# The RWKV branch prepared chunk by chunk without GpSimd, and another spread of the modulation tiles

## The chip, the core and the metric

The kernel runs on one core of a Trainium2 chip. A core has a matrix engine (TensorE, PE in the profile, with its weight loads as PEld), a vector engine (VectorE, DVE), an activation engine (ScalarE, ACT), GpSimd (POOL), and SyncE (SP), on which this kernel issues its transfers. Each engine works through its own queue in order; semaphores make one wait for another. The metric is the device time of one execution in microseconds (us); less is better.

## What is computed

Two layers of a transformer over 256 tokens of width 1024, batch 1, in float32. The first has stick-breaking attention and retention side by side; the second has a modulated norm, a mixer of latent attention (MLA) and an RWKV-7 recurrence joined by gates, and a PEER feed-forward over 16384 experts. Of the second layer the change touches these lines:

```python
mod = silu(c) @ w_ada + b_ada                     # 6 vectors of 1024: shifts, scales, gates
h = modulate(rms_norm(x, norm_mix), sh1, sc1)
proj = h @ w_in                                   # q_a, kv_a, k_rope, rwkv_in, gate_logits
...
p = p + (prev(p) - p) * mu                        # token_shift: the token before, mixed in
r, k, v, wd, ad, gd = split(p)
decay = exp(-exp(-softplus(-(decay_base + tanh(wd) @ w_decay_up)) - 0.5))
a = sigmoid(aaa_base + ad @ w_aaa_up)
kk = normalised(k * k_k);  k = k * (1 + (a - 1) * k_a);  b = kk * a
for t in range(S):                                # rwkv7_scan, per head
    state = state * w[t] - (state @ kk[t]) b[t]^T + v[t] k[t]^T
    y[t] = state @ r[t]
y = group_norm(y) + sum(r * k * r_k) * v          # the "bonus" term
o_rwkv = (y * g) @ w_o_rwkv
...
x = x + gt1 * ((sigmoid(gl[0]) * o_mla + sigmoid(gl[1]) * o_rwkv) @ w_out)
x = x + gt2 * peer(modulate(rms_norm(x, norm_ffn), sh2, sc2))
```

## The kernel before

**Weights.** Activations lie transposed (features on the 128 partitions, 256 tokens along the row). Weights come in tiles of 512 KB: `stream` (L76) issues the transfer on SP, and `halves` (L60) splits each tile in two halves (128x1024 to two of 128x512) and each of those into a high part (`whi`, a cast on ScalarE, L69) and a low part (`wlo`, a subtraction on VectorE, L71, or on GpSimd where `eng` says so, L73). `mm3` (L94 to L98) makes one product of three matmuls: high by high, high by low, low by high. `proj_t` (L101) runs whole projections in chunks of 256 output columns: 48 matmuls of 256 columns and two tiles a chunk. Its result in PSUM is `pj`; the narrow projections are `pn`, those of the gate logits `gj`.

**Order.** The program is written as Python generators, and a scheduler orders each engine's queue from it; `after(g, a, b)` is a hint that a is to stand behind b. In block 2, the loop over `rwkv` (L1073 on) advances three others at each of its yields: `mla` by `NML`, `gate_logits` (64 yields of 6 matmuls) by `NGT`, and the modulation by `NADA`. So gate matmuls fill the places where the recurrence waits.

**The modulation** (`load_mod`, L472) streams 48 tiles `adaw` of 128x1024, each weighed and summed by one VectorE instruction (L486, with its accumulator read). `keep_pace(g, rate)` lets so many of them go out per chunk. Block 1 does 21 of them, block 2 the other 27, partly while the recurrence runs, partly in its three output projections.

**The RWKV branch** (`rwkv`, L510). `shifted` (L523) copies a chunk's result to a buffer with a zero column ahead (`shb`, ScalarE), subtracts the two views (`shd`, GpSimd, L529), and mixes on VectorE (L532). All six chunks of k, r and v are projected first; then come the normalised key (`kkn`, `kk`), `bb` (L616 on GpSimd, L645), the key's weight (L624, `rwk`), the bonus (`bon` L628, matmul `bonp` L632), and the decays folded in (L643 to L646). Then `ntp` (transposes, L656), `mps` and `aps` (products within a chunk of 64 tokens, L674, L681), `mvp`. The triangular systems are inverted in five levels of two halves, ten steps: `bl` (mask product on GpSimd, L714), `zp` = X·bl (PE), Z (copy on ScalarE, L727), `yp` and `xp` (PE), X and Y (subtractions on VectorE, L733, L734). Then the states (`rhs`, `sap`, `ypp`, `u`) and the group norm, which ends in `orh` and `orl`, high and low part of the branch's output. MLA's queries, keys, scores and sums are `qh`, `mkh`, `qkp`, `sc`, `s`, `pp`, `ops`; its output `omh`, `oml`.

**The end of block 2.** Three projections, of MLA's output, of `orh`/`orl`, and of the merged `m2h`/`m2l`, then the norm ahead of the feed-forward (`sq`, `sqa`, `rms`, `nt`, `h3h`). Each chunk of them calls `keep_pace(g, 1)`.

In block 1, the four retention heads (`ret_head`, L387) are issued in a row behind the attention heads.

Of the kernel before, what the change touches and what calls it, by code (L numbers as in the profile page):

```python
# [100 lines left out]
def proj_t(g, w, xh, xl, chunks, nk=8, name="pj", eng=(None,)):  # L101

    nc = g.nc
    for i in chunks:
        bank = g.acc.tile([P, 2, T], F32, tag="acc", name=name)
        for k0, n, hi, lo in stream(g, w[i], nk, eng=eng):
            for c in range(2):
                cs = slice(c * P, (c + 1) * P)
# [4 lines left out]
        g.pm = i.ins
        yield bank
# [129 lines left out]
ADA_RATE = [0.5, 0.5, 0.5, 0, 0.5, 0.5, 0.5, 0, 0.5, 0.5]  # L244


def block1(g, a, xT):
    nc = g.nc
    with ExitStack() as es:
# [173 lines left out]
        turn, heads = {}, []  # L423
        for h in range(6):
            if h < 4:
                heads.append(ret_head(h, turn))
            for gen in reversed(heads):
                next(gen, None)
# [11 lines left out]
        obh, obl = b8("obh", F32R), b8("obl", F32R)  # L440
        gated(3, av, oah, oal)
# [9 lines left out]
        for i, bank in enumerate(proj_t(g, a["w_branch_sb"], oah, oal, range(4))):  # L451
            keep_pace(g, 0.75)
# [3 lines left out]
        for i, bank in enumerate(proj_t(g, a["w_branch_ret"], obh, obl, range(4))):  # L456
            keep_pace(g, 0.75)
# [5 lines left out]
        for i, bank in enumerate(proj_t(g, a["w_out"], mh, ml, range(4))):  # L463
            keep_pace(g, 0.75)
# [46 lines left out]
def rwkv(g, a, hh, hl, cp, b4, wk, og, ol):  # L511
# [60 lines left out]
    table(g, EXPLN)  # L572
    kT, rT, vT = t4("rwk"), t4("rwr"), t4("rwv")
    shifted(a["w2_rkv"], (2, 3), 4, [kT[:, i, :] for i in range(4)])
    shifted(a["w2_rkv"], (0, 1), 0, [rT[:, i, :] for i in range(4)])
    shifted(a["w2_rkv"], (4, 5), 8, [vT[:, i, :] for i in range(4)])
# [907 lines left out]
```

## Time and profile before

| | us |
|---|---|
| median of 3 runs (1485.04 to 1487.40) | 1486.97 |
| the profiled execution | 1486.97 |
| its span (first to last instruction) | 1485.1 |
| TensorE busy | 1423.0 (96%) |
| VectorE busy | 1127.4 (76%) |
| ScalarE busy | 795.6 (54%) |
| GpSimd busy | 122.0 (8%) |

The span lies 1.87 us under the execution's time. TensorE's granted clock is given as a share of 2.4 GHz: 1.00 is full, and a stretch at 1.2 GHz counts as 0.50, so that busy time multiplied by the mean clock is what the same matmuls take at full clock. The program's places in time: block 1 up to about 360 us; the first `lor` matmul (the decay's second layer) at 382.2; `ntp` at 441.6; the first `zp` at 467.3; the first matmul on `omh` at 592.0, on `orh` at 607.2; the last on `m2h`/`m2l` at 650.5; the first on `h3h` at 659.6. From there to the end it is the feed-forward.

### The profile page before, as it was taken

The page shows a single profiled execution, that of the slowest core. Times are in us where ns is not written, and L with a number is a line of the kernel's source. Part 1 is how long each engine was busy: PE and PEld are TensorE (multiplying, and loading weights), DVE is VectorE, ACT ScalarE, POOL GpSimd, SP SyncE. Part 2 cuts the span into 40 slices and gives each one's busy share as a digit, 9 for nine tenths or more (in the row PEclk, how much of TensorE's full clock was granted, in tenths as well). Part 3 has the DMA queues.
Part 4 walks back from the last instruction along what each step waited for, and adds up shares of the span by engine and source line. Part 5 has one row for each costly group of instructions (what it writes and reads, how often), then busy time and mean ns, then how long its engine had stood idle before and what let it go on. Part 6 is the DMA issues. An engine that isn't in the chain of part 4 may idle for free.

```text
span 1485.1 us, 29346 instructions
## 1 busy us (share of the span) xinstructions
PE 1423.0 (96%) x11284; PEld 1324.6 (89%) x11284; DVE 1127.4 (76%) x2411; ACT 795.6 (54%) x1606; POOL 122.0 (8%) x99
## 2 busy tenths in 40 slices
PE   7999999998988999789999998999999999999997
PEld 6999989998977888779999998999998888888886
DVE  8768678688677764988998898989996666666665
ACT  6655557545663445445555555555445555555553
POOL 3012012000153422000000000000000000000001
PEclk9999999999989999889999999999999999999999
DMA  7656526775640343755555554454445566666564
GB/s 252 213 173 194 187 79 204 228 257 187 190 134 18 107 143 100 235 186 177 172 177 182 183 171 145 141 158 155 159 151 172 189 192 193 196 193 194 194 192 135
DMA packets 73723, 256.46 MB, mean 173 GB/s; under 512 B 9328, under 2 KB 10992, under 8 KB 73584
## 3 DMA queue, kind: packets, MB, share of 16 engines
q1 hardware_dynamic: 73584, 254.60, 53.5%
q8 instruction: 88, 1.44, 0.4%
q14 instruction: 51, 0.42, 0.1%
HBM read 253.52 MB, written 1.05 MB: 171 GB/s over the span
## 4 chain that ended last, share of the span: by engine, by line
PE 53%; DVE 1%; issue 0%; POOL 0%; POOLq 0%
PE dn L96 8%; PE dn L98 8%; PE dn L97 8%; PE upp L1307 8%; PE upp L1308 8%; PE upp L1311 8%; PE gps L1280 2%; PE pj L97 1%; PE pj L98 1%; PE pj L96 1%; PE sps L1144 0%; DVE wlo L71 0%; DVE eq L1272 0%; DVE gt L1274 0%; POOL y L1357 0%
## 5 line engine op out<-in xcount | busy, mean ns | idle before, releaser
L69 ACT CAST whi<-eraw 128x512 fp32r<-128x512 f32 x512 | 311.1, 620 | 346.0 <-PE upp L1308 152.0
L71 DVE TENSOR_TENSOR wlo<-eraw,whi 128x512 fp32r<-128x512 f32 x512 | 346.8, 690 | 168.7 <-ACT whi L69 107.8
L69 ACT CAST whi<-wraw 128x512 fp32r<-128x512 f32 x336 | 206.2, 618 | 183.4 <-PE pj L97 98.5
L96 PE MATMUL dn<-h3h,whi 128*128 128x256 f32 x1024 | 293.7, 287 | 0.0
L98 PE MATMUL dn<-h3h,wlo 128*128 128x256 f32 x1024 | 291.8, 285 | 0.0
L97 PE MATMUL dn<-h3l,whi 128*128 128x256 f32 x1024 | 290.9, 284 | 0.0
L71 DVE TENSOR_TENSOR wlo<-wraw,whi 128x512 fp32r<-128x512 f32 x304 | 212.5, 712 | 80.9 <-ACT whi L69 75.9
L97 PEld LDWEIGHTS dn<-h3l,whi 128*128 128x128 f32 x1024 | 197.5, 193 | 0.0
L96 PEld LDWEIGHTS dn<-h3h,whi 128*128 128x128 f32 x1024 | 197.5, 193 | 0.0
L98 PEld LDWEIGHTS dn<-h3h,wlo 128*128 128x128 f32 x1024 | 197.3, 193 | 0.0
L1308 PE MATMUL upp<-whi,wl 128*128 128x512 f32 x512 | 158.9, 390 | 0.0
L1311 PE MATMUL upp<-wlo,wh 128*128 128x512 f32 x512 | 157.9, 390 | 0.0
L98 PE MATMUL pj<-hh,wlo 128*128 128x256 f32 x496 | 141.1, 286 | 2.5 <-DVE wlo L71 2.5
L96 PE MATMUL pj<-hh,whi 128*128 128x256 f32 x496 | 141.2, 286 | 2.2 <-ACT hh L58 1.5
L97 PE MATMUL pj<-hl,whi 128*128 128x256 f32 x496 | 141.5, 286 | 1.0 <-DVE hl L59 0.9
L1307 PE MATMUL upp<-whi,wh 128*128 128x512 f32 x512 | 138.6, 391 | 0.0
L1311 PEld LDWEIGHTS upp<-wlo,wh 128*128 128x128 f32 x512 | 96.1, 188 | 20.1
L1308 PEld LDWEIGHTS upp<-whi,wl 128*128 128x128 f32 x512 | 95.9, 188 | 19.6
L1307 PEld LDWEIGHTS upp<-whi,wh 128*128 128x128 f32 x512 | 95.8, 188 | 19.6
L96 PEld LDWEIGHTS pj<-hh,whi 128*128 128x128 f32 x496 | 95.7, 193 | 3.1 <-ACT hh L58 1.7
L98 PEld LDWEIGHTS pj<-hh,wlo 128*128 128x128 f32 x496 | 95.3, 193 | 3.5 <-DVE wlo L71 3.3
L97 PEld LDWEIGHTS pj<-hl,whi 128*128 128x128 f32 x496 | 95.5, 193 | 2.1 <-DVE hl L59 1.9
(477 smaller groups left out, 2825.2 us busy)
## 6 DMA issues: line engine op xcount, KB each, us to landing
eraw<-in_e_down_dram SPq DMA_DIRECT2D x128, 512.0 KB, 4.0
eraw<-in_e_up_dram SPq DMA_DIRECT2D x128, 512.0 KB, 4.5
wraw<-in_w_in_dram SPq DMA_DIRECT2D x80, 512.0 KB, 4.1
adaw<-in_w_ada_dram SPq DMA_DIRECT2D x48, 512.0 KB, 5.0
wraw<-in_w_out_dram SPq DMA_DIRECT2D x16, 512.0 KB, 4.7
wraw<-in_w_gate_dram SPq DMA_DIRECT2D x16, 512.0 KB, 4.0
wraw<-in_w_query_dram SPq DMA_DIRECT2D x16, 512.0 KB, 4.2
wraw<-in_w_rkv_dram SPq DMA_DIRECT2D x12, 512.0 KB, 4.5
```

The lines of the kernel that those rows point to most:

```text
L69: nc.scalar.copy(hi[:, :m], raw[:, o:o + m])
L71: nc.vector.tensor_tensor(lo[:, :m], raw[:, o:o + m], hi[:, :m], op=ALU.subtract)
L96: nc.tensor.matmul(out, lh, rh, start=start, stop=False)
L97: nc.tensor.matmul(out, lh, rl, start=False, stop=False)
L98: return nc.tensor.matmul(out, ll, rh, start=False, stop=stop)
L1280: nc.tensor.matmul(ps[:, t, :], eq[:, 0, pr, :, o], gt[:, i, pr, :, o], start=i == 0, stop=i == 1)
L1307: nc.tensor.matmul(o, wh[:, ts], hi, start=J == 0, stop=False)
L1308: nc.tensor.matmul(o, wl[:, ts], hi, start=False, stop=False)
L1311: nc.tensor.matmul(up_ps[2 * tt + d0 // 4], wh[:, ts], lo, start=False, stop=J == NJ - 1)
```

## The change

1. `shifted` keeps no buffer: ScalarE writes (1 − mu) times the chunk out of PSUM, VectorE adds mu times the token before, also out of PSUM. It is a generator now: k, r and v are prepared in stages between chunks (`k_stage`, `r_stage`, `v_stage`), and `behind` puts the small matmuls (`lor`, `kkn`, `bonp`) behind the middle of the chunk then running.
2. GpSimd has no work left in block 2's mixer. Seven `shd` go away; `bb`, ten `bl`, the 32 `wlo` halves of the gate logits and the first X and Y products (four on GpSimd, now in quarters) go to VectorE. The tile A and its mask go away.
3. `ADA_RATE` and the rates in block 1's projections change: 31 modulation tiles there, not 21. Block 2 does 14 in the recurrence (rates 0.5 and 0.4 after a start without any), none in the first two output projections, 3 in the last.
4. Block 1's retention heads are issued between the chunks that make block 1's gates.
5. `NGT` gives 42 gate matmuls ahead of `ntp` (78 before), 72 between `ntp` and `zp` (none before), and six after each `zp` and six after each `xp` (before: twelve after each `zp`).

```diff
-ADA_RATE = [0.5, 0.5, 0.5, 0, 0.5, 0.5, 0.5, 0, 0.5, 0.5]
+ADA_RATE = [0.5, 0.5, 0.75, 0.25, 0.75, 0.75, 0.5, 0.25, 1, 1]
...
+                next(ret, None)
...
         for i, bank in enumerate(proj_t(g, a["w_branch_sb"], oah, oal, range(4))):
-            keep_pace(g, 0.75)
+            keep_pace(g, 1)
...
         for i, bank in enumerate(proj_t(g, a["w_out"], mh, ml, range(4))):
-            keep_pace(g, 0.75)
+            keep_pace(g, 0.5)
...
         for b, bank in enumerate(proj_t(g, w, hh, hl, chunks)):
-            buf = wk.tile([P, 2, T + 1], F32, tag="shb", name="shb")
-            nc.vector.memset(buf[:, :, 0:1], 0.0)
-            nc.scalar.copy(buf[:, :, 1:], bank)
-            d = wk.tile([P, 2, T], F32, tag="t512", bufs=4, name="shd")
-            nc.gpsimd.tensor_tensor(d, buf[:, :, 0:T], buf[:, :, 1:], op=ALU.subtract)
             for j in range(2):
                 i = b * 2 + j
-                nc.vector.scalar_tensor_tensor(dsts[i], d[:, j, :], g.vec[:, o_mu + i0 + i:o_mu + i0 + i + 1],
-                                               buf[:, j, 1:], op0=ALU.mult, op1=ALU.add)
+                nc.scalar.activation(dsts[i], bank[:, j, :], AF.Copy, scale=mu1[:, i0 + i:i0 + i + 1])
+                nc.vector.scalar_tensor_tensor(dsts[i][:, 1:T], bank[:, j, 0:T - 1],
+                                               g.vec[:, o_mu + i0 + i:o_mu + i0 + i + 1], dsts[i][:, 1:T],
+                                               op0=ALU.mult, op1=ALU.add)
+            yield b * 2
...
+    next(k_chunks)
+    k_stage(0)
+    r_chunks = shifted(a["w2_rkv"], (0, 1), 0, [rT[:, i, :] for i in range(4)])
+    next(r_chunks)
+    k_stage(2)
+    next(r_chunks)
+    r_stage(0)
+    v_chunks = shifted(a["w2_rkv"], (4, 5), 8, [vT[:, i, :] for i in range(4)])
+    next(v_chunks)
+    r_stage(2)
     yield
...
+    next(v_chunks)
+    v_stage(0)
+    v_stage(2)
     yield
...
             bl = wk.tile([P, 8, 64], F32, tag="bl", bufs=2, name="bl")
-            nc.gpsimd.tensor_tensor(bl, MB[tt][:, :, 0:64], lvl[:, l, :].unsqueeze(1).broadcast_to([P, 8, 64]),
+            nc.vector.tensor_tensor(bl, MB[tt][:, :, 0:64], lvl[:, l, :].unsqueeze(1).broadcast_to([P, 8, 64]),
                                     op=ALU.mult)
...
-NGT = [4, 4, 4, 2] + [2, 0] * 10 + [2] * 11 + [4, 4]
-
-NADA = [0] * 8 + [0.5] * 27 + [0] * 2
+NGT = [4, 4] + [2] * 6 + [1, 1] * 10 + [2, 1] + [1, 2, 1] * 3 + [4, 5]
+
+NADA = [0] * 8 + [0.5] * 20 + [0.4] * 11 + [0] * 2
...
-        for k0, n, hi, lo in stream(g, a["w2_gate"][i], eng=(nc.gpsimd,)):
+        for k0, n, hi, lo in stream(g, a["w2_gate"][i]):
...
         for i, bank in enumerate(proj_t(g, a["w_o_mla_2"], omh, oml, range(4), nk=4)):
-            keep_pace(g, 1)
...
         for i, bank in enumerate(proj_t(g, a["w_o_rwkv_2"], orh, orl, range(4), nk=4)):
-            keep_pace(g, 1)
...
         for i, bank in enumerate(proj_t(g, a["w_out_2"], mh, ml, range(4))):
-            keep_pace(g, 1)
+            keep_pace(g, 0.75)
```

**Order on TensorE ahead of the recurrence.** The bonus matmul and what follows it, before:

```order
3090 L1049 MATMUL gj<-h2h,whi 128x256
3091 L1052 MATMUL gj<-h2l,whi 128x256
3092 L1053 MATMUL gj<-h2h,wlo 128x256
3093 L632 MATMUL bonp<-bon,c_4662 128x512 x2
3094 L656 MATMUL ntp<-perm,bb 128x128 x8
3095 L656 MATMUL ntp<-perm,rwk 128x128 x8
3096 L656 MATMUL ntp<-perm,rwv 128x128 x8
```

and after the change (`pj` there is the last chunk of v):

```order
3034 L97 MATMUL pj<-h2l,whi 128x256
3035 L98 MATMUL pj<-h2h,wlo 128x256
3036 L949 MATMUL cqp<-perm,qn 128x128 x3
3037 L663 MATMUL bonp<-bon,c_4692 128x512 x2
3038 L1080 MATMUL gj<-h2h,whi 128x256
3039 L1083 MATMUL gj<-h2l,whi 128x256
3040 L1084 MATMUL gj<-h2h,wlo 128x256
```

Before, all gate matmuls of this place stood ahead of the bonus, and `ntp` right behind it; now it stands behind the last chunk of v, and 18 gate matmuls lie between it and `ntp`.

**Order on VectorE in the recurrence**, some two steps of it, before:

```order
478 L984 TENSOR_TENSOR s<-sc,cau 128x512
479 L733 TENSOR_TENSOR X<-X,xp 128x512
480 L734 TENSOR_TENSOR Y<-Y,yp 128x512
481 L990 TENSOR_REDUCE m<-s 128x4
482 L486 SCALAR_TENSOR_TENSOR adaw,perm<-adaw,silc 128x1024
483 L994 RECIPROCAL ri<-sm 128x4
484 L995 TENSOR_TENSOR s<-s,ri 128x512
485 L733 TENSOR_TENSOR X<-X,xp 128x512
486 L734 TENSOR_TENSOR Y<-Y,yp 128x512
```

and after:

```order
551 L495 SCALAR_TENSOR_TENSOR adaw,perm<-adaw,silc 128x1024
552 L764 TENSOR_TENSOR X<-X,xp 128x512
553 L765 TENSOR_TENSOR Y<-Y,yp 128x512
554 L59 TENSOR_TENSOR oml<-ops,omh 128x2x128
555 L1015 TENSOR_TENSOR s<-sc,cau 128x2x128
556 L745 TENSOR_TENSOR bl<-MB_5551,c_4692 128x512
557 L1021 TENSOR_REDUCE m<-s 128x2
558 L171 TENSOR_SCALAR gm<-gj 128x512
559 L71 TENSOR_TENSOR wlo<-wraw,whi 128x512
560 L1025 RECIPROCAL ri<-sm 128x2
561 L1026 TENSOR_TENSOR s<-s,ri 128x512
562 L495 SCALAR_TENSOR_TENSOR adaw,perm<-adaw,silc 128x1024
```

Between one pair of X and Y and the next there now stand a `bl`, a `wlo` and a modulation tile on the same queue.

**Order on VectorE from the group norm to `orl`**, before:

```order
617 L486 SCALAR_TENSOR_TENSOR adaw,perm<-adaw,silc 128x1024
618 L71 TENSOR_TENSOR wlo<-wraw,whi 128x512
619 L1092 TENSOR_TENSOR gm<-gm,pj 128x512
620 L814 TENSOR_SCALAR yb<-yb,perm 128x256 x2
621 L71 TENSOR_TENSOR wlo<-wraw,whi 128x512
622 L817 TENSOR_TENSOR yb<-yb,gt 128x512
623 L486 SCALAR_TENSOR_TENSOR adaw,perm<-adaw,silc 128x1024
624 L71 TENSOR_TENSOR wlo<-wraw,whi 128x512
625 L1092 TENSOR_TENSOR gm<-gm,pj 128x512
626 L71 TENSOR_TENSOR wlo<-wraw,whi 128x512
627 L816 TENSOR_TENSOR yb<-yb,bon 128x512
628 L59 TENSOR_TENSOR orl<-yb,orh 128x512
```

and after:

```order
699 L843 TENSOR_TENSOR yb<-yb,gnr 128x512
700 L71 TENSOR_TENSOR wlo<-wraw,whi 128x512
701 L845 TENSOR_SCALAR yb<-yb,perm 128x256 x2
702 L1122 TENSOR_TENSOR gm<-gm,pj 128x512
703 L71 TENSOR_TENSOR wlo<-wraw,whi 128x512
704 L847 TENSOR_TENSOR yb<-yb,bon 128x512
705 L848 TENSOR_TENSOR yb<-yb,gt 128x512
706 L71 TENSOR_TENSOR wlo<-wraw,whi 128x512
707 L1122 TENSOR_TENSOR gm<-gm,pj 128x512
708 L843 TENSOR_TENSOR yb<-yb,gnr 128x512
709 L71 TENSOR_TENSOR wlo<-wraw,whi 128x512
710 L59 TENSOR_TENSOR orl<-yb,orh 128x512
```

No modulation tile stands in this chain any more; the instructions of the chain itself are the same.

## Rows read from the trace of the kernel before

**Rows 1.** The page: busy time of each engine, and VectorE's undisturbed low halves.

```profile
PE 1423.0 (96%) x11284; PEld 1324.6 (89%) x11284; DVE 1127.4 (76%) x2411; ACT 795.6 (54%) x1606; POOL 122.0 (8%) x99
...
L71 DVE TENSOR_TENSOR wlo<-eraw,whi 128x512 fp32r<-128x512 f32 x512 | 346.8, 690 | 168.7 <-ACT whi L69 107.8
```

**Rows 2.** Windows: length, busy (count) of PE PEld DVE ACT POOL, clock, DMA.

```profile
382.20:441.60 59.40, 52.28 (x399) 48.37 (x399) 43.22 (x69) 37.50 (x81) 23.76 (x16) 0.93 0.50 155
441.60:467.27 25.67, 21.73 (x301) 18.51 (x300) 20.43 (x57) 9.69 (x24) 7.52 (x6) 0.89 0.02 8
467.27:592.00 124.73, 119.09 (x1746) 103.78 (x1747) 77.71 (x173) 62.08 (x146) 42.13 (x30) 1.00 0.35 109
592.00:607.20 15.20, 12.52 (x100) 11.84 (x98) 15.12 (x27) 9.43 (x16) 0.00 (x0) 1.00 0.63 210
607.20:625.20 18.00, 14.98 (x108) 14.78 (x109) 16.01 (x29) 6.63 (x11) 0.00 (x0) 0.81 0.70 228
625.20:650.50 25.30, 23.50 (x182) 23.00 (x181) 22.22 (x41) 11.83 (x20) 0.00 (x0) 0.93 0.73 251
650.50:659.60 9.10, 2.22 (x11) 1.26 (x10) 7.80 (x19) 2.78 (x7) 0.67 (x1) 0.78 0.64 202
...
680.00:1485.00 805.00, 792.23 (x5468) 729.22 (x5466) 623.39 (x1435) 419.05 (x873) 4.15 (x3) 0.99 0.54 174
```

**Rows 3.** Waits of TensorE from 360 to 660: total, times, longest (us).

```profile
PE bonp L632 <- DVE bon L628: 6.1, 1, 6.1
PE pj L96 <- ACT h3h L58: 5.0, 1, 5.0
...
PE pj L97 <- DVE orl L59: 3.0, 1, 3.0
PE pj L96 <- ACT orh L58: 2.7, 1, 2.7
PE mvp L696 <- DVE A L683: 2.6, 1, 2.6
PE qkp L969 <- DVE mkh L963: 2.2, 2, 1.3
...
PE pj L97 <- DVE m2l L59: 1.7, 1, 1.7
PE qkp L969 <- DVE qh L884: 1.7, 2, 1.0
```

**Rows 4.** Groups of GpSimd by line: busy us, mean ns, idle before.

```profile
L73 POOL TENSOR_TENSOR wlo<-wraw,whi 128x512 fp32r<-128x512 f32 x32 | 45.5, 1426 | 66.8 <-ACT whi L69 64.9 <-PE gj L1053 1.5
L714 POOL TENSOR_TENSOR bl<-MB,c 128x512 f32<-128x512 f32 x10 | 13.8, 1381 | 37.7 <-PE zp L721 18.2 <-DVE ssq L945 15.5 <-DVE MB L676 4.0
...
L616 POOL TENSOR_TENSOR bb<-kk,al 128x1024 f32<-128x1024 f32 x1 | 3.4, 3442 | 0.8 <-DVE kk L613 0.8
```

**Rows 5.** Groups of VectorE by line and shape from 360 to 600.

```profile
L995 DVE TENSOR_TENSOR s<-s,ri 128x512 f32<-128x512 f32 x6 | 6.6, 1104 | 0.1
...
L645 DVE TENSOR_TENSOR bb<-bb,en 128x1024 f32<-128x1024 f32 x1 | 2.3, 2269 | 2.3 <-POOL bb L616 2.3
...
L646 DVE TENSOR_TENSOR rwk<-rwk,en 128x1024 f32<-128x1024 f32 x1 | 1.2, 1210 | 0.0
```

**Rows 6.** Timeline of VectorE at three modulation tiles: start, length, [idle before].

```profile
602.23 1.23 DVE L486 SCALAR_TENSOR_TENSOR adaw<-adaw,silc 128x1024 f32<-128x1024 f32 x1
603.37 0.09 DVE L486 DVE_READ_ACCUMULATOR adaw<-adaw,silc 128x1 f32 x1
...
650.13 1.23 DVE L486 SCALAR_TENSOR_TENSOR adaw<-adaw,silc 128x1024 f32<-128x1024 f32 x1
...
654.91 1.22 DVE L486 SCALAR_TENSOR_TENSOR adaw<-adaw,silc 128x1024 f32<-128x1024 f32 x1 [0.95 <-DMA adaw<-in_w_ada_dram]
```

**Rows 7.** Windows, columns as in rows 2: the densest transfers of block 1.

```profile
320.00:340.00 20.00, 20.00 (x170) 20.00 (x168) 18.02 (x32) 10.31 (x17) 0.00 (x0) 1.00 0.82 266
```

**Rows 8.** The tile zp: the copy that reads it (min/median/max ns, first and last start).

```profile
L727 ACT COPY Z<-zp x10: 570/586/591, 468.5 to 530.5; 128x512 f32<-128x512 f32 x10
```

More of the change, by code (lines that the diff above doesn't have):

```diff
@@ L413, in ret_head @@
                 if j == 0:
-                    after(g, i.ins, turn[1])
+                    after(g, i.ins, g.pm)
             r = wk.tile([P, T], F32, tag="t256", bufs=3, name="rr")
@@ L421, in ret_head, with ret_heads @@
                                                op0=ALU.mult, op1=ALU.mult)
[L423 to L428, printed above, removed]
+        def ret_heads():
+            heads = []
+            for h in range(6):
+                if h < 4:
+                    heads.append(ret_head(h))
+                for gen in reversed(heads):
+                    next(gen, None)
+                yield
         def gated(i0, x, hi, lo):
@@ L440, in block1 @@
         obh, obl = b8("obh", F32R), b8("obl", F32R)
+        ret = ret_heads()
+        next(ret)
         gated(3, av, oah, oal)
@@ L557, in rwkv, with behind @@
     load(g, eye, a["c_eye"])
-    load(g, slow, a["c_slow"])
     nc.vector.memset(smask, 1.0)
     nc.vector.memset(smask[:, ::64], 0.0)
+    kT, bb = t4("rwk"), t4("bb")
+    k_chunks = shifted(a["w2_rkv"], (2, 3), 4, [kT[:, i, :] for i in range(4)])
+    next(k_chunks)
+    def behind(i):
+        after(g, i.ins, g.mid)
     sg, al = t4("sgm"), t4("al")
@@ L567, in rwkv @@
                 c = c0 + j
-                nc.tensor.matmul(ps[:, j, :], up[r0:r0 + 64, c * P:(c + 1) * P], wdad[r0:r0 + 64, :], start=True, stop=True)
+                behind(nc.tensor.matmul(ps[:, j, :], up[r0:r0 + 64, c * P:(c + 1) * P], wdad[r0:r0 + 64, :],
+                                        start=True, stop=True))
             for j in range(2):
                 act(g, dst[:, c0 + j, :], ps[:, j, :], AF.Sigmoid, bias=col(g, nm, c0 + j))
+    ka1 = wk.tile([P, 4], F32, tag="ka1", bufs=1, name="ka1")
+    o = VEC["k_a_2"][0]
+    nc.vector.tensor_scalar(ka1, g.vec[:, o:o + 4], -1.0, 1.0, op0=ALU.mult, op1=ALU.add)
+    kh = t4("kh")
+    for c in range(4):
+        nc.scalar.activation(kh[:, c, :], al[:, c, :], AF.Identity, scale=col(g, "k_a_2", c), bias=ka1[:, c:c + 1])
     table(g, EXPLN)
[L573 to L576, printed above, removed]
     cu = t4("cu")
@@ L606, in rwkv @@
         ps = g.aux.tile([P, 2, T], F32, tag="aux", name="kkn")
-        nc.tensor.matmul(ps, bones, sq, start=True, stop=True)
+        behind(nc.tensor.matmul(ps, bones, sq, start=True, stop=True))
+        rn = wk.tile([P, 2, T], F32, tag="t512", bufs=4, name="rn")
+        nc.vector.tensor_scalar(rn, ps, 1e-24, None, op0=ALU.max)
+        act(g, rn, rn, AF.Ln)
+        act(g, rn, rn, AF.Exp, scale=-0.5)
+        kk = wk.tile([P, 2, T], F32, tag="kk", bufs=1, name="kk")
+        for j in range(2):
+            nc.vector.scalar_tensor_tensor(kk[:, j, :], kT[:, c + j, :], col(g, "k_k_2", c + j), rn[:, j, :],
+                                           op0=ALU.mult, op1=ALU.mult)
@@ L630, in rwkv, with v_stage @@
-    for c in range(0, 4, 2):
+        nc.vector.tensor_tensor(kh[:, cs, :], kh[:, cs, :], en[:, cs, :], op=ALU.mult)
+    def v_stage(c):
         ps = g.aux.tile([P, 2, T], F32, tag="aux", name="bonp")
-        nc.tensor.matmul(ps, bones, bon[:, c:c + 2, :], start=True, stop=True)
+        behind(nc.tensor.matmul(ps, bones, bon[:, c:c + 2, :], start=True, stop=True))
         nc.vector.tensor_tensor(bon[:, c:c + 2, :], ps, vT[:, c:c + 2, :], op=ALU.mult)
-    yield
-    kr = b4.tile([P, 4, 4, 2, 64], F32, tag="b8s", bufs=1, name="kr")
```

102 lines of the change are left out of this document (47 added, 55 removed).

## Prediction

> **What bounds the kernel now.** First the page's busy line [rows 1]: TensorE is busy 96% of the span, VectorE 76%, GpSimd 8%. That is a matrix-bound kernel, and a change that removes no matmul can only win where TensorE stands still or runs slowly. So the second view is the windows by stage [rows 2]; for each stage I multiply TensorE's busy time by the granted clock, which is what its matmuls take at full clock, and set it against the stage's length. From 680 us on, 792.2 × 0.99 = 784 of 805: little to win, and the change does not touch it. Three stages of block 2 are different:
> - `lor` to `ntp`: 52.28 × 0.93 = 48.6 of 59.40, so 10.8 us lost;
> - `ntp` to `omh` (two rows): 21.73 × 0.89 + 119.09 = 138.4 of 150.40, 12.0 lost;
> - `omh` to `h3h` (four rows): 12.52 + 14.98 × 0.81 + 23.50 × 0.93 + 2.22 × 0.78 = 48.2 of 67.60, 19.4 lost.
>
> That is 42 us in all. The third view, TensorE's waits [rows 3], says for whom: one of 6.1 us ahead of `bonp` in the first stage, the A, `mkh` and `qh` waits (2.6 + 2.2 + 1.7 = 6.5) in the second, `orh`, `orl`, `m2l`, `h3h` (2.7 + 3.0 + 1.7 + 5.0 = 12.4) in the third. The rest is slow clock: the low clocks of rows 2 stand in the very stages that have a long wait.
>
> **Part 1: preparation in stages (`lor` to `ntp`).** Before, the chain k to `kk` to `bb` to `bon` runs after the last chunk of v, and GpSimd is in it: `bb` takes 3.44 us there, and the VectorE instruction that follows takes 2.27 where its twin takes 1.21 [rows 4, 5]. The gate matmuls run out and TensorE stands 6.1 us. In the new order the bonus products of r stand on VectorE while v's chunks run on TensorE (two chunks of 48 matmuls, at the pace of rows 7, 20.00/170 = 0.118 us each, 11 us), so the 6.1 us go, and with them most of the slow clock that follows (52.28 − 48.6 = 3.7 us). What is late next: the first chunk of r. Ahead of its low halves VectorE has the four scans of the decay, two whole-width instructions and two half-width ones; at 0.69 a 512-wide one at most [rows 1] and 1.21 a whole one [rows 5] that is 4 × 0.69 + 2 × 1.21 + 2 × 0.69 = 6.6 us, against one chunk of cover (5.7 us) and two or three low halves that must come before TensorE can start. I take a wait of 2 to 3 us there. Of the 10.8 lost, about 4 stay: gain 7. Bounds: the wait costs nothing and the clock stays high, 10; it is twice as long and slows the clock again, 4.
>
> **Part 2: the recurrence (`ntp` to `omh`).** VectorE takes over here ten `bl`, some 28 of the 32 gate low halves (42 of the gate's 384 matmuls come ahead of `ntp`, and a half serves 12) and the first products. Rows 1 give 0.69 for the 512-wide instruction that takes GpSimd 1.38 to 1.43 [rows 4]: 10 × 0.69 + 28 × 0.69 + about 3 = 29 us more on VectorE. What it gets back is the time by which its instructions are stretched while GpSimd runs: the six `s` products cost 1.104 us [rows 5] where the like costs 0.69, so 2.5 in all. GpSimd runs 36 instructions here [rows 2]; if half of them hold up one VectorE instruction by half their 1.4 us, that is 13, an estimate that I take. Its busy time goes from 20.43 + 77.71 = 98 to about 114 of 150 us [rows 2]: 76%, not a bound by the sum, though it is an in-order queue. Modulation tiles are the same load here (13 before, 14 now). Then the fillers. The copy Z that separates `zp` from `yp` takes 0.586 us [rows 8] and a hand-over; twelve gate matmuls (1.4 us) covered it, six (0.7) just do or fall short by up to 0.3 us, ten times: up to 3 lost. The other six now cover `xp` to X. For it: the 72 gate matmuls among `mps`, `aps` and `mvp` fill just the stretch in which A, `mkh` and `qh` were waited for [rows 3] and the clock was 0.89 [rows 2]. Of 12.0 lost I let 10 remain: gain 2. Bounds: half of it goes, +6; VectorE's queue holds up the chain by 0.8 us in each of ten steps, −6 (with the 2 of gain).
>
> What these rows show, VectorE instructions with two inputs in SBUF stretched beside a reading GpSimd, is also a rule of the Trainium skill (SBUF — State Buffer, Who interferes with whom): the two share a port pair, and the loser blocks for the whole instruction. The trace agrees (2.27 against 1.21), and by that rule all of the stretch goes with GpSimd's work, as assumed.
>
> **Part 3: the end of block 2 (`omh` to `h3h`).** Nothing hides VectorE here: in 592.0 to 607.2 it is busy 15.12 of 15.20 us [rows 2], and its queue from group norm to `orl` holds four modulation tiles; one costs 1.14 us from its start to that of its accumulator read [rows 6]. In the new order none stands there. With three fewer ahead of `orh` it comes 3.4 us earlier, which ends its 2.7 us of wait; with four fewer the first `orl` comes 4.6 earlier, and TensorE, which by then has done its two matmuls on `orh`, waits 1.3 us for it and no more. Together 5.7 become 1.3: 4.4 gained. The clock of 0.81 behind these waits cost 14.98 × 0.19 = 2.8 us; I count it as gone. Four tiles ahead of `m2l` go too, and with them its 1.7 us and the 0.93 clock (23.50 × 0.07 = 1.6). In the norm two tiles [rows 6] stand in the chain: at 650.13 ahead of the last x update (1.14), at 654.91 ahead of `nt`, with a wait for its transfer (0.95 + 1.22, of which I take 1.25, since `nt` needs the last sum as well). In the new order the last tile comes before that update and none before `nt`: 2.4. Sum 4.4 + 2.8 + 1.7 + 1.6 + 2.4 = 12.9; I take 12.5. Bounds: all and the norm's wait shrinks by the clock too, 14.5; the slow clock stays, 8.
>
> **Part 4: block 1.** Ten more tiles there: 10 × 1.22 us of VectorE, beside a TensorE that runs without loss at 320 to 340 with VectorE busy 18.0 of 20 [rows 7], and 5.2 MB more of transfers. In the branch projections the need at rate 1 is three tiles of 0.524 MB in 48 × 0.118 = 5.7 us, 276 GB/s; rows 7 show 266 with no loss, at 0.82 of the engines' time. So it just fits: 0, bounds −4 and +3. The tiles are issued on SP ahead of weights, so a late one holds up what is queued behind it. The retention heads still stand in one block on TensorE, a gate chunk or two later, hundreds of matmuls ahead of their use: nothing.
>
> **Sum.** 7 + 2 + 12.5 + 0 = 21.5. The profiled execution took 1486.97 us, span 1485.1 and 1.87 around it, and is itself the median. 1486.97 − 21.5 = 1465.5.
>
> **The rivals.**
> - *Only the end gains.* Preparation and recurrence trade GpSimd's waits for waits in VectorE's longer queue, r's first chunk above all: parts 1 and 2 cancel, 1486.97 − 12.5 = 1474.5. For it: VectorE would be busy 76% on average, more in the steps. Against: `bonp`'s wait is one of order, not of load.
> - *Block 1 runs out of transfer rate.* At 251 GB/s, the densest of rows 2, a chunk needs 6.3 us in place of 5.7; over 16 chunks 9 us: 1474.5 as well. Against: rows 7.
> - *The stretch is not GpSimd's doing.* Then VectorE gets nothing back, is busy 127 of 150 us, and the recurrence loses 8: 1486.97 − 7 − 12.5 + 8 = 1475.5. Against: L645 beside L646.
> - *The recurrence hangs on VectorE: slower.* In each of the ten steps a `bl` (0.69), a `wlo` (0.69) and a modulation tile (1.22) stand on one queue between X and X; if all of it lies in the chain, 2.6 × 10 = 26 us are lost: 1486.97 − 7 − 12.5 + 26 = 1493.5. It decides from about 2 us a step (19.5 / 10). For it: X and Y wait behind what is queued ahead whoever needs it. Against: the two halves alternate, so that a late X has the other half's step as cover.
>
> On this last one a page speaks against the change: the Trainium skill (Perfetto Trace Analysis, Optimizing Scalar/DVE Operations) has it that a saturated VectorE may be relieved by moving work to GpSimd, and adds that the shared port may take that back. By it the reverse move costs where VectorE is the limit; no stage between `ntp` and `omh` shows it saturated before.
>
> **How the numbers follow.** Forecast 0.52, only the end 0.18, block 1 0.12, no relief 0.06, recurrence slower 0.09, anything else 0.03. Low end: the best bounds, 10 + 6 + 14.5 + 3 = 33.5, so 1453. High end: the middle rivals and some more, 1480; the slower case lies outside. A measurement of this kernel tells about 0.2% (3 us) from no change; faster than that 0.87, within it 0.04, slower 0.09.
>
> **What would show it.** Right: no wait ahead of `bonp`, `lor` to `ntp` in about 52 us; `omh` to `h3h` in about 55 with no wait above 2 us but the norm's; `wlo` on VectorE at 0.69 there and `s` near 0.7; block 1 at its old length. Wrong: TensorE waiting for X, Y or `bl` in most steps between 465 and 530, weight waits in block 1's projections, or an `orh` as late as before.

## The result, and the profile after

The changed kernel takes 1462.75 us (median of 4, 1460.88 to 1464.86) against 1486.01 for the kernel before beside it: a ratio of 0.9843, 95% interval 0.9831 to 0.9854. Forecast was 1465.5, range 1453 to 1480. The profiled execution took 1462.46, span 1460.6, so 24.5 us less than the profiled span before.

The page's busy line [rows 1] now reads

```profile
PE 1420.6 (97%) x11284; PEld 1321.2 (90%) x11284; DVE 1140.0 (78%) x2462; ACT 807.8 (55%) x1613; POOL 46.8 (3%) x45
```

The same matmuls in less time. TensorE's busy time fell by 2.4 us, and the time in which it stood idle (span less busy) from 62.1 to 40.0, so 22 of the 24.5 us are idle time. The mean granted clock went from 0.982 to 0.992 (view of the cores), that is from 26.7 to 11.7 us of missing clock over the span. The two can't be added up, since a slow clock costs nothing while TensorE stands idle. Two slow stretches of the kernel before, ahead of `ntp` and behind `orh` (columns as in rows 2):

```profile
433.71:441.60 7.89, 3.52 (x4) 1.41 (x5) 7.09 (x12) 2.01 (x7) 3.94 (x3) 0.50 0.53 161
607.79:614.62 6.83, 3.90 (x18) 3.90 (x19) 4.84 (x9) 1.24 (x2) 0.00 (x0) 0.50 0.92 303
```

At half clock, half of the busy time is what the clock cost, 1.8 and 2.0 us by that estimate; the rest of these stretches is idle.

The windows that answer to rows 2, cut at the same events (first `lor`, `ntp`, `zp`, matmul on `omh`, on `orh`, on `m2h`, last on `m2h`, first on `h3h`):

```profile
379.00:434.90 55.90, 52.66 (x409) 49.12 (x409) 44.99 (x101) 38.67 (x89) 0.00 (x0) 1.00 0.50 157
434.90:464.90 30.00, 30.00 (x374) 25.86 (x372) 23.76 (x75) 17.09 (x40) 0.00 (x0) 1.00 0.19 63
464.90:581.50 116.60, 116.15 (x1707) 99.84 (x1706) 80.91 (x181) 56.39 (x133) 0.00 (x0) 1.00 0.37 118
581.50:593.90 12.40, 12.40 (x101) 11.92 (x100) 12.29 (x23) 8.76 (x15) 0.00 (x0) 1.00 0.38 128
593.90:606.20 12.30, 11.98 (x98) 11.57 (x97) 11.15 (x19) 6.66 (x11) 0.00 (x0) 1.00 0.54 173
606.20:629.10 22.90, 22.90 (x193) 22.90 (x192) 20.78 (x37) 12.66 (x21) 0.17 (x1) 1.00 0.66 216
629.10:635.60 6.50, 2.34 (x12) 1.38 (x10) 4.77 (x13) 2.79 (x7) 0.45 (x1) 0.87 0.49 161
```

The clock is 1.00 up to the norm, and between `omh` and the last `m2h` TensorE is busy but for 0.3 us. TensorE's waits in the second layer's mixer, 360 to 640 us (answering to rows 3):

```profile
PE pj L96 <- ACT h3h L58: 4.0, 1, 4.0
PE pn L130 <- DVE wlo L71: 2.4, 2, 1.9
PE lor L586 <- ACT lora L164: 1.3, 1, 1.3
PE pj L96 <- DVE rn L639: 0.6, 1, 0.6
...
PE pj L97 <- DVE orl L59: 0.2, 1, 0.2
```

The waits for `bonp`, A, `mkh`, `orh`, `m2l` are gone; what is left is the norm (`h3h`) and, new, a narrow projection that waits for its low half.

| from, to | before | after | equal work | forecast |
|---|---|---|---|---|
| start to first matmul on `h2h` | 363.1 | 364.3 | 1.2 lost | 0 |
| to `lor` | 19.2 | 14.6 | 0 | |
| `lor` to `ntp` | 59.4 | 55.9 | 4.0 gained | 7 |
| `ntp` to `omh` | 150.4 | 146.6 | 8.0 gained | 2 |
| `omh` to `h3h` | 67.6 | 54.1 | 13.5 gained | 12.5 |
| `h3h` to the end | 825.5 | 825.0 | 0.5 gained | 0 |

"Equal work" allows for what the events let pass: 40 matmuls of k's first chunk stood ahead of `lor` before and stand behind it now (40 × 0.118 = 4.7 us), and 36 gate matmuls have moved from ahead of `ntp` to behind it (4.2 us). Six small `cqp` matmuls (some 0.6 us), which moved the other way, are not allowed for.

### The profile page after: what moved, and what is told of

Its sections match the earlier page's. It is cut to its first block, busy times and chain, and to the rows that moved or that the text cites. A ratio compares the mean times of both kernels' runs of the same rounds, so it can differ in the third digit from the quotient of the medians.

```text
span 1460.6 us, 29215 instructions
## 1 busy us (share of the span) xinstructions
PE 1420.6 (97%) x11284; PEld 1321.2 (90%) x11284; DVE 1140.0 (78%) x2462; ACT 807.8 (55%) x1613; POOL 46.8 (3%) x45
## 4 chain that ended last, share of the span: by engine, by line
PE 54%; DVE 2%; issue 0%; POOL 0%; POOLq 0%; DVEq 0%
PE dn L96 8%; PE dn L98 8%; PE dn L97 8%; PE upp L1336 8%; PE upp L1337 8%; PE upp L1340 8%; PE gps L1309 2%; PE pj L97 1%; PE pj L98 1%; PE pj L96 1%; PE sps L1173 0%; DVE wlo L71 0%; DVE eq L1301 0%; DVE gt L1303 0%; PE gtp L1357 0%
## 5 line engine op out<-in xcount | busy, mean ns | idle before, releaser
L69 ACT CAST whi<-eraw 128x512 fp32r<-128x512 f32 x512 | 318.1, 622 | 336.7 <-PE upp L1337 146.5
L71 DVE TENSOR_TENSOR wlo<-wraw,whi 128x512 fp32r<-128x512 f32 x336 | 238.1, 720 | 73.9 <-ACT whi L69 69.7
L1337 PEld LDWEIGHTS upp<-whi,wl 128*128 128x128 f32 x512 | 95.8, 188 | 19.8
```

What stands on the lines that cost most here:

```text
L69: nc.scalar.copy(hi[:, :m], raw[:, o:o + m])
L71: nc.vector.tensor_tensor(lo[:, :m], raw[:, o:o + m], hi[:, :m], op=ALU.subtract)
L1337: nc.tensor.matmul(o, wl[:, ts], hi, start=False, stop=False)
```

## The experiments

Medians, each beside runs of the kernel before on the same chip. The last two columns are read from each timeline: the first matmul on `h2h` (all of block 1 and the step to block 2), and from there to the first on `h3h`, a stretch that holds the same matmuls in all of them.

| kernel | us | ratio to before, interval | to `h2h` | `h2h` to `h3h` |
|---|---|---|---|---|
| before | 1486.0 | | 363.1 | 296.5 |
| changed | 1462.75 | 0.9843 (0.9831 to 0.9854) | 364.3 | 271.3 |
| e1_gpsimd_back | 1465.48 | 0.9864 (0.9844 to 0.9884) | 364.8 | 277.3 |
| e2_fill_early | 1463.25 | 0.9853 (0.9834 to 0.9873) | 362.9 | 273.8 |
| e3_mod_back | 1473.83 | 0.9925 (0.9903 to 0.9947) | 358.5 | 286.2 |
| e4_mod_alone | 1480.71 | 0.9971 (0.9958 to 0.9983) | 367.8 | 286.7 |
| e5_ret_block | 1470.07 | 0.9891 (0.9873 to 0.9910) | 368.3 | 276.3 |
| e6_merge_half | 1459.13 | 0.9820 (0.9803 to 0.9837) | 360.6 | 273.6 |
| e8_cover_twelve | 1456.77 | 0.9805 (0.9788 to 0.9821) | 362.2 | 268.1 |
| e10_both_old | 1470.52 | 0.9902 (0.9866 to 0.9939) | 363.8 | 277.7 |
| e11_half_and_twelve | 1458.27 | 0.9807 (0.9791 to 0.9824) | 359.5 | 272.1 |
| e12_engines_alone | 1465.80 | 0.9865 (0.9848 to 0.9881) | 363.0 | 276.7 |
| e13_split_alone | 1486.49 | 1.0002 (0.9991 to 1.0012) | 361.2 | 300.1 |
| e14_without_staging | 1459.61 | 0.9826 (0.9811 to 0.9841) | 360.2 | 272.5 |

Kernels with the same code up to `h2h` differ there by up to 2.6 us (changed, e1, e2, e8, e10: 362.2 to 364.8). From `h2h` to `h3h` they differ by more: 271.3, 273.6 and 276.3 us in three kernels with the same code there (changed, e6, e5), 268.1 and 272.1 in two others (e8, e11). Smaller differences of one profile show nothing by themselves. The scheduler works out all orders anew after any edit, so an edit in one place can move instructions in another.

**The modulation tiles.** e3 puts the old spread back into the changed kernel, e4 takes the new one into the kernel before.

```diff
-ADA_RATE = [0.5, 0.5, 0.75, 0.25, 0.75, 0.75, 0.5, 0.25, 1, 1]
+ADA_RATE = [0.5, 0.5, 0.5, 0, 0.5, 0.5, 0.5, 0, 0.5, 0.5]
...
-NADA = [0] * 8 + [0.5] * 20 + [0.4] * 11 + [0] * 2
+NADA = [0] * 8 + [0.5] * 27 + [0] * 6
...
         for i, bank in enumerate(proj_t(g, a["w_o_rwkv_2"], orh, orl, range(4), nk=4)):
+            keep_pace(g, 1)
```

(the diff of e3; the other rates go back likewise, and e4 is the reverse on the kernel before)

> The changed kernel with the modulation tiles spread as before (21 in block 1, rate 1 in all three output projections). My theory of the end of block 2: orh, orl and m2l are waited for again, omh to h3h goes from 54 back to about 66 us, block 1 gets back about 2: 1472 to 1475. Rival (the end gained because the recurrence's work on VectorE ends earlier, not by the tiles): at most 4 us slower than the changed kernel, 1463 to 1467.

> The kernel before with the new spread of the modulation tiles alone. My theory: omh to h3h shrinks from 67.6 to about 55 us and block 1 loses about 2: 1474 to 1477. Rival (the chain to orl was late by GpSimd's and the recurrence's delays): 1481 to 1486.

e3: 1473.83, as expected. From `omh` to `h3h` it needs 67.0 us in place of 54.1, and the waits of rows 3 are back (TensorE's waits of e3, 570 to 650 us):

```profile
PE pj L96 <- ACT h3h L58: 4.1, 1, 4.1
PE pj L96 <- ACT orh L58: 2.7, 1, 2.7
PE pj L97 <- DVE orl L59: 2.7, 1, 2.7
PE rms L213 <- ACT sq L208: 2.4, 1, 2.4
PE pj L97 <- DVE m2l L59: 1.9, 1, 1.9
```

e4: 1480.71, less of a gain than expected. The end itself does what was said, 55.2 us in place of 67.6; but block 1 takes 4.7 us longer (367.8), and `ntp` to `omh` 3.0 (153.3). So the term of part 3 is shown from both sides, 13 and 12 us, with and without the other parts, and so is what part 4 had at 0: ten tiles in block 1 cost 5.8 (e3 beside the changed kernel) and 4.7 (e4 beside before).

**The retention heads.** e5 issues them in a row again.

```diff
-                next(ret, None)
...
-        ret = ret_heads()
-        next(ret)
+        for _ in ret_heads():
+            pass
```

> The changed kernel with the retention heads issued in a row again, as before. My prediction's term (the heads' place is worth nothing): within 1.5 us of the changed kernel. Rival, from the windows of the kernel with the old spread of modulation tiles, where block 1 up to its branch projections took 283.2 us in place of 287.0 before: the place is worth some 4 us, since heads in a row make the gate chunks behind them wait for VectorE; with ten more tiles there it is worth at least that: 1466 to 1469, with waits for wlo or sg between 205 and 230 us.

1470.07: the rival. Block 1 takes 368.3 in place of 364.3, and the waits stand where the rival put them (e5, then the changed kernel, 180 to 280 us):

```profile
PE pj L98 <- DVE wlo L71: 3.4, 4, 2.7
PE avp L363 <- DVE sbw L339: 1.9, 1, 1.9
PE pj L96 <- DVE ro L423: 1.0, 1, 1.0
```

```profile
PE pj L98 <- DVE wlo L71: 1.8, 4, 0.8
PE pj L96 <- ACT whi L69: 1.7, 1, 1.7
```

e3 beside the kernel before says the same with the old spread: 358.5 against 363.1. So the heads' place is worth some 4 us in block 1. The 5 us that e5 loses between `h2h` and `h3h`, where its code is that of the changed kernel, are not explained; its order there is another.

**Rate 1 in block 1.** The wait for `whi` in the fence above stands at 263.9. ScalarE's timeline there (changed kernel; start, length, [idle before]):

```profile
257.02 1.14 ACT L69 CAST whi<-wraw 128x512 fp32r<-128x512 f32 x2 [2.71 <-DMA wraw<-in_w_in_dram]
...
259.72 1.28 ACT L148 ACT_TABLE_LOAD   x1
261.01 2.30 ACT L164 ACTIVATE ea<-pj,perm 128x256 f32<-128x256 f32 x6
263.17 2.21 ACT L69 CAST whi<-wraw 128x512 fp32r<-128x512 f32 x4
```

ScalarE waits 2.71 us for the weights, and the next casts then fall behind a table load and six sigmoids. e6 lowers the rate in that projection and raises it in the output projection:

```diff
-ADA_RATE = [0.5, 0.5, 0.75, 0.25, 0.75, 0.75, 0.5, 0.25, 1, 1]
+ADA_RATE = [0.5, 0.5, 0.75, 0.25, 0.75, 0.75, 0.5, 0.25, 0.5, 1]
...
-            keep_pace(g, 0.5)
+            keep_pace(g, 1)
```

> The changed kernel with rate 0.5 in place of 1 in the first merge projection of block 1, and rate 1 in place of 0.5 in its output projection; 31 tiles in block 1 as changed. Theory: the tiles at rate 1 make the weights of that projection late, at 257 to 268 us of the changed kernel, where ScalarE's casts then fall behind a table load and six sigmoids: about 3 us of wait and slow clock go, 1459 to 1461, unless the output projection's tiles hold up its norm by as much. Rival (the wait is the table load's own, whatever the tiles): 1462 to 1464.

1459.13, as the theory says: `h2h` comes 3.7 us earlier, and from 180 to 280 us one group of waits is left:

```profile
PE pj L98 <- DVE wlo L71: 0.8, 2, 0.5
```

e11, with the same rates, comes to `h2h` at 359.5, and e14 at 360.2. So modulation tiles did hold up weights in block 1, as a rival of the prediction had it, at one place and for some 3 us; whether for want of transfer rate or because they stand ahead of the weights on SP was not separated. In the branch projections, for which the rival was priced, TensorE stays busy at rate 1 (the changed kernel from 280 to 320 us: busy 40.00 of 40.00, 282 and 280 GB/s).

**Engines and fillers in the changed kernel.** e1 gives the gate's low halves and `bl` back to GpSimd, e2 moves the 72 gate matmuls ahead of `ntp`, e10 does both.

```diff
-        for k0, n, hi, lo in stream(g, a["w2_gate"][i]):
+        for k0, n, hi, lo in stream(g, a["w2_gate"][i], eng=(nc.gpsimd,)):
...
-            nc.vector.tensor_tensor(bl, MB[tt]
+            nc.gpsimd.tensor_tensor(bl, MB[tt]
...
-NGT = [4, 4] + [2] * 6 + [1, 1] * 10 + [2, 1] + [1, 2, 1] * 3 + [4, 5]
+NGT = [10, 10] + [0] * 6 + [1, 1] * 10 + [2, 1] + [1, 2, 1] * 3 + [4, 5]
```

> The changed kernel with the gate's low halves and the ten bl given back to GpSimd; everything else as changed. Stretch theory: VectorE's instructions beside GpSimd get longer again (the s products from 0.69 to about 1.1 us), and the eight microseconds that the stretch from ntp to omh gained at equal work are mostly lost: 1467 to 1471, with qh, mkh or bl among TensorE's waits again. Filler theory (it is the 72 gate matmuls put among mps, aps and mvp that gained it, whoever makes the low halves): within 2 us of the changed kernel, 1461 to 1465.

> The changed kernel with the 72 gate matmuls that stand between ntp and zp moved ahead of ntp, VectorE and GpSimd as changed. Stretch theory: the chain from ntp to zp is short enough without fillers, within 2 us of the changed kernel. Filler theory: TensorE waits there again for the products and for mkh and qh, and the clock falls behind it: 1468 to 1473.

> The changed kernel with the gate's low halves and bl on GpSimd again and the 72 gate matmuls ahead of ntp again, both at once. Each alone cost 0.5 to 3 us. If the two cover for each other (either a VectorE without stretch or fillers under its waits), both together cost 6 to 9: 1468 to 1472. If they add up: 1465 to 1467, and what the stretch from ntp to omh gained comes from the products made in quarters and the staged preparation.

e1, 1465.48: between the two; 6.0 us more from `h2h` to `h3h`, which is little over the differences between kernels of the same code there. Of the waits that it was to bring back, those for `qh` and `mkh` came, and one for `qn` (e1, 360 to 640 us; the changed kernel has none of the three):

```profile
PE qkp L1000 <- DVE qh L915: 1.2, 1, 1.2
PE cqp L949 <- DVE qn L945: 1.1, 2, 0.8
...
PE qkp L1000 <- DVE mkh L994: 0.6, 1, 0.6
```

VectorE's instructions got longer again, but not the `s` products that I had named (groups of VectorE, 360 to 600 us, e1 and then the changed kernel):

```profile
L495 DVE SCALAR_TENSOR_TENSOR adaw<-adaw,silc 128x1024 f32<-128x1024 f32 x14 | 20.0, 1426 | 0.1
...
L1026 DVE TENSOR_TENSOR s<-s,ri 128x512 f32<-128x512 f32 x6 | 4.1, 691 | 0.2
...
L925 DVE TENSOR_TENSOR ry<-rs 128x4 f32<-128x4 f32 x4 | 2.8, 698 | 0.3 <-ACT rs L164 0.3
```

```profile
L495 DVE SCALAR_TENSOR_TENSOR adaw<-adaw,silc 128x1024 f32<-128x1024 f32 x14 | 17.0, 1216 | 0.1
...
L1026 DVE TENSOR_TENSOR s<-s,ri 128x512 f32<-128x512 f32 x6 | 4.1, 690 | 0.2
...
L925 DVE TENSOR_TENSOR ry<-rs 128x4 f32<-128x4 f32 x4 | 0.6, 152 | 0.0
```

It strikes what happens to stand beside GpSimd: in e1 three modulation tiles, for which nobody waits, and above all the small instructions of MLA's norms, queries and keys. Of the VectorE instructions of 360 to 600 us, 26 in the kernel before are over 0.25 us longer than the shortest of their operation and shape, by 23 us together; in e1 it is 18, by 16 us (12 for MLA, 3 for the tiles), and in the changed kernel none. Each of the 26 and of the 18 overlaps an instruction on GpSimd. e2, 1463.25: the filler theory falls as the cause of the gain. Its signs are there in small, waits of 0.4 and 0.3 us and a clock of 0.83 from `ntp` to `zp`, but the median is that of the changed kernel. e10, 1470.52, has a median and a spread (1464.7 to 1474.7) that fit both of its cases: not settled.

**The parts alone.** e12 gives all of the mixer's GpSimd work (`shd`, `bb`, `bl`, first X and Y, the gate's low halves) to VectorE in the kernel before: six times `nc.gpsimd` to `nc.vector`, and no other change.

```diff
-        for k0, n, hi, lo in stream(g, a["w2_gate"][i], eng=(nc.gpsimd,)):
+        for k0, n, hi, lo in stream(g, a["w2_gate"][i]):
...
-    nc.gpsimd.tensor_tensor(bb, kk, al, op=ALU.mult)
+    nc.vector.tensor_tensor(bb, kk, al, op=ALU.mult)
```

> The kernel before with all GpSimd work of the mixer (shd, bb, bl, first X and Y products, the gate's low halves) given to VectorE and nothing else. Theory (engines and staging each gain their part of lor to omh, some 5 and some 6 us at equal work): 1479 to 1482, with the wait ahead of bonp shorter but still there. Rival (the engines are the whole of it, the staging only makes room): 1473 to 1476. Second rival (without the staging VectorE's queue loses what the stretch gives back): 1485 to 1489.

1465.80, far outside my theory and better than the first rival: this one edit has seven eighths of the whole change's gain (20.6 of 23.3 us by the medians beside each). No VectorE instruction of 360 to 600 us is 0.25 us longer than the shortest of its operation and shape, as in the changed kernel. `bonp`'s wait is halved, without any staging; `orh` is named once, for 1.4 us (e12's waits, 360 to 650 us):

```profile
PE bonp L632 <- DVE bon L628: 2.9, 1, 2.9
PE pj L97 <- DVE m2l L59: 2.4, 2, 1.5
PE pp L1001 <- ACT orh L58: 1.4, 1, 1.4
```

The gain of 20.6 us can have two sources, which e12 removes together: the VectorE instructions that GpSimd lengthens, and GpSimd's own slower pace where its result is waited for. The chain to `bonp` has both (VectorE's timeline of the kernel before, then of e12):

```profile
423.14 3.29 DVE L613 SCALAR_TENSOR_TENSOR kk<-rwk,perm,rn 128x256 f32<-128x256 f32 x4 [1.12 <-ACT rn L162]
...
435.16 3.57 DVE L628 SCALAR_TENSOR_TENSOR bon<-rwr,perm,rwk 128x256 f32<-128x256 f32 x4
```

```profile
425.84 1.22 DVE L616 TENSOR_TENSOR bb<-kk,al 128x1024 f32<-128x1024 f32 x1
...
428.11 1.22 DVE L645 TENSOR_TENSOR bb<-bb,en 128x1024 f32<-128x1024 f32 x1
...
431.58 1.66 DVE L628 SCALAR_TENSOR_TENSOR bon<-rwr,perm,rwk 128x256 f32<-128x256 f32 x4
```

From `kk` to the end of `bon` it is 15.6 us before and 10.7 in e12. GpSimd's own pace is 2.2 of it (`bb` 3.44 [rows 4] against 1.22); the lengthened `kk`, L645 and `bon` are 4.5 (3.29, 2.27 [rows 5] and 3.57 against 1.74, 1.22 and 1.66); what VectorE took over takes some back. TensorE itself named GpSimd once before, for 1.0 us (`gj` for a `wlo`). How the whole 20.6 us divides between the two was not tested.

Windows of e12, `lor` to `ntp`, `ntp` to `zp` and `zp` to `omh` (some of MLA's last matmuls come behind the third):

```profile
381.20:434.40 53.20, 50.28 (x400) 47.71 (x400) 42.63 (x78) 37.29 (x81) 0.00 (x0) 1.00 0.50 162
434.40:454.70 20.30, 18.88 (x297) 15.46 (x296) 17.96 (x64) 8.72 (x25) 0.00 (x0) 1.00 0.20 63
454.70:572.70 118.00, 116.46 (x1738) 102.68 (x1739) 88.14 (x208) 60.87 (x141) 0.00 (x0) 1.00 0.34 113
```

So the stage that the staging was meant for gains 6.2 us without it (59.4 to 53.2, the same matmuls), more than in the changed kernel. The recurrence is no quicker than the changed kernel's at equal work: `ntp` to `orh` takes 156.6 us against 159.0, with 36 gate matmuls (4.2 us) fewer and six `cqp` more.

e14 adds to e12 the new spread of tiles (with e6's rates) and the heads between the gate chunks: everything but the staging and its fillers.

> The kernel before with GpSimd's work of the mixer on VectorE, the new spread of the modulation tiles (rate 0.5 in the first merge projection, 1 in block 1's output projection) and the retention heads between the gate chunks; no staged preparation, the old fillers. If the parts gain in different stages and add up (engines some 15 us in lor to omh, tiles some 12 in omh to h3h, block 1 between -2 and +1): 1451 to 1456, faster than the changed kernel, and the staging and its fillers cost it 4 us or more. If the tiles' gain is the same as that of the engines, by the end no longer being late: 1460 to 1465.

1459.61, between the two cases: the parts add up only partly. From `h2h` to `h3h`: 296.5 before, 286.7 with the tiles alone (e4), 276.7 with the engines alone (e12), 272.5 with both (e14), 271.3 with the staging on top (changed). The tiles save 6.4 us from `omh` to `h3h` on top of e12 (67.0 to 60.6), where they saved 12.4 alone: in e12 and e14 twelve of MLA's last matmuls stand ahead of those on `orh`. The last step, of 1 us, holds the staging, its fillers, their split and the rates of e6, and is smaller than the differences between kernels of the same code. The nearest pair is e14 and e11, which has e6's rates and unsplit fillers as well: 272.5 and 272.1, medians 1459.61 and 1458.27, intervals that overlap. No gain of the staging is shown once GpSimd is out. With `bl` and the gate's low halves on GpSimd (e1, 57 of the 76 us of work that e12 takes off it) it may be larger: 277.3 against 286.7 in e4.

**The split fillers.** e8 puts twelve gate matmuls after each `zp` again, e13 splits them in the kernel before.

```diff
-NGT = [4, 4] + [2] * 6 + [1, 1] * 10 + [2, 1] + [1, 2, 1] * 3 + [4, 5]
+NGT = [4, 4] + [2] * 6 + [2, 0] * 10 + [2, 1] + [1, 2, 1] * 3 + [4, 5]
```

> The changed kernel with twelve gate matmuls after each zp and none after xp, as before. My term: six cover the copy Z just or fall short by up to 0.3 us in each of ten steps, so twelve gain up to 3 us unless X is late without cover: 1460 to 1463. Rival (X and Y now wait behind bl, wlo and a modulation tile, and need the six): 1464 to 1468.

> The kernel before with the twelve gate matmuls of each step split in six after zp and six after xp, nothing else. Theory (each change between a 64x64 group and 256-column matmuls costs TensorE some 0.3 us, as the timeline of the changed kernel shows at 484.0 to 485.0, whatever VectorE's load): ntp to omh 3 to 5 us longer, 1488 to 1491. Rival (the split cost the changed kernel its time only through Z's copy waiting on its loaded engines): within 1.5 us of before.

> The two single edits that were faster than the changed kernel, together: rate 0.5 in the first merge projection with rate 1 in the output projection, and twelve gate matmuls after each zp with none after xp. If they add up (3.6 and 6.0 us by the medians, 2 and 4 by the stages that they touch): 1453 to 1457. If the second already held the first's gain by chance of order: 1456 to 1459.

e8 is the fastest of all, 1456.77: 6 us under the changed kernel, more than the 3 that I had for the cover. `zp` to `omh` takes 112.8 us in place of 116.6. Little of it is the copy Z (0.8 us of waits for it in the changed kernel, none in e8). TensorE's timeline of the changed kernel shows more:

```profile
484.05 0.38 PE L1080 MATMUL gj<-h2h,whi 128*128 128x256 f32 x1
484.27 0.28 PE L1083 MATMUL gj<-h2l,whi 128*128 128x256 f32 x1
484.39 0.28 PE L1084 MATMUL gj<-h2h,wlo 128*128 128x256 f32 x1
484.51 0.28 PE L1080 MATMUL gj<-h2h,whi 128*128 128x256 f32 x1
484.63 0.28 PE L1083 MATMUL gj<-h2l,whi 128*128 128x256 f32 x1
484.74 0.28 PE L1084 MATMUL gj<-h2h,wlo 128*128 128x256 f32 x1
484.95 0.68 PE L752 MATMUL zp<-X,bl 64*64 64x64 f32 x14
```

The first of six follows a small 64x64 matmul, and its successor starts 0.22 us behind it, not 0.12; the next small one starts 0.21 behind the last. Six matmuls take 0.90 us in place of 0.72, and ten more lumps of six some 2 us (the expectation of e13 had 0.3 us at each change; it is 0.1). Counted from `zp` to `omh`, such changes between differently tiled matmuls are 101 in the changed kernel and 79 in e8; but e11, with 80, needs 115.4 us there: what the changes cost lies between its 1.2 us and e8's 3.8. In e13 `ntp` to `omh` grows from 150.4 to 153.5, as expected, but the median does not move: that the split costs by itself is seen in the stage and not in the total, and stays open; by the median alone its rival holds. e11 joins e6 and e8 and does not add up (1458.27): block 1 keeps e6's gain (359.5), `zp` to `omh` does not keep e8's. So what makes e8 the fastest stays open.

## Why the prediction was right, and where its steps were not

The total came within 3 us of the forecast (1462.75 against 1465.5), in part by luck: part 1 gained 3 us less than forecast and part 2 six more, and the zero of part 4 was a loss and a gain.

**What bounds the kernel**: the three stages with idle time and slow clock are those that gained; block 1 lost 1.2 us, the rest moved by 0.5. Two readings of rows 2 were too simple. Of the 42 us, 31 are idle time and 11 slow clock by the windows, and the waits named make 25 of the 31; so not all of "the rest" was slow clock. And busy time multiplied by the mean clock of a window charges the slow clock of idle time as well: by the slow stretches themselves (TensorE busy in 3.52, 2.35, 3.21, 3.90 and 3.35 us of them) the clock cost 8.2 us, not 11.

**Part 3** (12.5) was sized right, 13.5 measured and 12 to 13 by e3 and e4: tiles in the chain to `orl` and in the norm, and the slow clock behind the waits. One term of it was too large: the clock behind `orh` cost 2.0 us, not 2.8.

**Part 1** (7) gained 4.0. The wait ahead of `bonp` went, as said; but what came late next was not r's first chunk (0.6 us, the wait for `rn`) but the narrow projections behind it (2.4) and `lor` itself (1.3). What stays, 55.90 − 52.66 = 3.2 us idle at full clock, is near the 4 forecast; mis-sized is the 10.8, whose 3.7 of slow clock were 1.8 (3.52 of busy time at half clock). And the reason given, that `bonp`'s wait is one of order and not of load, is half of it: e12 leaves the order, halves the wait, and gains 6.2 in this stage. That the staging gained the 4.0 is not shown.

**Part 2** (2) gained 8.0. The step that failed is its balance: I let ten of twelve lost us remain for fear of VectorE's queue. The stretch came back whole (none left; it was 14.7 us in this stage before, where I had 13), and busy with 23.76 + 80.91 = 105 us VectorE had less to do than the 114 that I counted. The fillers, in contrast, may have cost more than the 3 us that I feared for the cover: e8 takes off 6, but beside e6 the same edit (e11) takes off 1. And the reason given, the 72 matmuls under A, `mkh` and `qh`, is shown wrong by e2, which does without them at no loss that its median shows.

**Part 4** (0) was the sum of two terms that I had both at nothing: ten tiles cost 5 to 6 us, the heads between the gate chunks give back 4. "Hundreds of matmuls ahead of their use" looked at who waits for the heads; it did not look at who waits behind them on VectorE, the gate chunks with their `wlo` and `sg`.

**The separation of the parts** failed as well: 7, 2 and 12.5 were added as if independent. From `h2h` to `h3h` the engines alone gain 19.8, the tiles alone 9.8, both together 24.0 and the whole 25.2.

The rivals: that the stretch is not GpSimd's doing is excluded (none after, in e12 or in e14, and back in e1); "the recurrence hangs on VectorE" too (waits for X, Y or `bl` in no step); "only the end" by the 4.0 and 8.0 us ahead of it; of "block 1", some 3 of its 9 us are seen, at another place.

## What to carry to other kernels

A second engine that is busy 8% of the time can still set the pace, by lengthening the instructions of the engine that others wait for, beside being slow where it stands in a chain itself: list one engine's instructions by shape and compare the longest with the shortest before reordering anything. Then try the smallest edit alone; here it held most of the gain, and no gain of the restructuring around it is shown. When a block of small work is called free because its result is needed late, look also at what stands behind it in the same queues.

## What was not expected of the hardware

In e1, VectorE's instruction on 128x4 elements took 0.698 us on average in place of 0.152, and the one on 128x1024 1.426 in place of 1.216: what is added does not go with the instruction's own size. One on 128x4 in the kernel before took 1.23 us (at 478.9), near the 1.27 of the GpSimd instruction that started beside it. This goes with the Trainium skill (SBUF — State Buffer, Who interferes with whom), where the port pair that the two engines share is an exclusive lock. With GpSimd's own pace, it is how 76 of GpSimd's 122 us of work could be worth 20 us. Nor are all of the lengthened ones of the kind with two inputs that the prediction names: two of the 26 and four of the 18 (`rx`, `qn`) are TENSOR_SCALAR, with one input tensor.

TensorE lost about 0.1 us at each change between 64x64 matmuls and 128x128 ones (0.22 and 0.21 us from start to start in the timeline of e8's section, where 0.12 is usual). The Trainium skill (TensorEngine Tiling (Array Packing), Key Properties) says that a change of tiling mode drains the engine; the trace agrees in that every such change costs time, and puts a number on it: some 0.2 us for each lump of fillers between 64x64 groups.
